# Two FFN up-projections as a seven-product block scheme, with the down-projection as a phase of its own

## The chip, the cores and the metric

The kernel runs on one core of a Trainium2 chip. Five engines take part. TensorE (PE in the rows, PEld its weight loads) multiplies, VectorE (DVE), ScalarE (ACT) and GpSimd (POOL) work element by element, and SyncE (SP) issues nearly all transfers. The metric is the device time of one execution in microseconds, as the median of several executions.

## The reference

A decoder trunk over 1024 tokens of 1024 values: two layers, each a mixer (differential attention with spatial gating in layer 0, a width-31 convolution module in layer 1) and then a gated FFN, which the change is about:

```python
def conv_ffn(h, w_up, dw_w, dw_b, w_down):
    hh = causal_dwconv(h @ w_up, dw_w, dw_b)   # width 3 over tokens, [1024, 5632]
    a, gate = jnp.split(hh, 2, axis=-1)
    return (a * jax.nn.silu(gate)) @ w_down    # [1024, 2816] @ [2816, 1024]

for l in range(2):
    h = rms_norm(x, norm_mix_g[l])
    x = x + (even_mixer if l == 0 else odd_mixer)(h, ...)
    x = x + conv_ffn(rms_norm(x, norm_ffn_g[l]), ffn_w_up[l], ffn_dw_w[l], ffn_dw_b[l], ffn_w_down[l])
return rms_norm(x, final_norm_g)
```

## The kernel before

**Products.** All is in fp32. Every factor is split into two parts hi and lo (`split_hi_lo`: a cast on ACT or DVE, a subtraction on POOL or DVE), and a product of 128x128 weights with 512 columns is three matmuls (hi hi, hi lo, lo hi; `PASSES`). The tokens are two chunks of 512. `stream` loads 512 KB of a weight into a `raw` tile (3 of them), and splits each half into a `hl` tile (8 of them).

**FFN.** A hidden group is two pairs of channel tiles (`GRP` = 2), 11 groups for each chunk and layer. For each channel tile `chan_mm` (L283) makes 24 matmuls into one PSUM bank; `up` evacuates them with the width-3 convolution (ACT L535, DVE L538 for the bank's two other taps, DVE L541 for the edge that comes from the chunk before). `up_a` multiplies by the gate (L555) and splits the product. The group is then pending: after the next group's first pair, `down_steps` (L589) multiplies it with its rows of `w_down`, 12 matmuls into a bank for each token tile and half, and adds each bank into the residual stream `xr` in SBUF (DVE L593). Weights are loaded anew for each chunk.

**Order.** Steps are Python closures; `interleave(main, shadow)` spreads one list over another, and a scheduler then fixes each engine's order. The FFN groups are the `main` that other work is spread over: attention of chunk 1 (`att_steps`) over groups 0 to 6 of layer 0, and in layer 1 the width-31 convolution (`dw_steps`: 22 taps on DVE, L713, and 7 on ACT and POOL for each of 8 channel tiles and chunk) with its layer norm (`ln_steps`) over nine groups of layer 0's chunk 1 and seven groups of layer 1's chunk 0:

```python
interleave(ffn_steps(0, 1, hF0, range(2, NG), pend) + down_steps(pend),
           dw_steps(ys[0]) + spread(ln_steps(0, ys[0], acT), 32), 0.0, 0.9)
```

**PSUM.** Eight banks: one `bank2` of two banks, two `sbank`, four `bank`.

## Time and profile before

| what | value |
|---|---|
| three runs | 2275.6, 2278.47, 2281.07 us (median 2278.47) |
| profiled execution | span 2279.0 us, the time that the sums below go by |
| granted TensorE clock | 0.992 on the mean |
| busy: PE, PEld, DVE, ACT, POOL | 97%, 80%, 73%, 45%, 43% of the span |
| transfers | 258.53 MB, 113 GB/s over the span |

The profile is one execution. Its page gives the busy share of each engine; views of the trace give stretches, groups of like instructions, and the chain of work that ended last.

### The profile page before, as it was taken

The numbers are of one execution on the slowest core, as the hardware profiler recorded it, in microseconds if no ns is written. First come the engines' busy times: TensorE is split into PE (matmuls) and PEld (weight loads), VectorE is DVE, ScalarE is ACT, GpSimd is POOL, SyncE is SP. The second block draws the span as 40 slices with busy tenths as digits, with TensorE's granted clock in tenths as the row PEclk, the third lists the DMA queues.
The fourth block names the chain that finished last, engine by engine and source line by source line (L and its number), as shares of the span: only waits on it lengthen the run. The fifth ranks groups of instructions, "written<-read, shape, count | busy, mean of one in ns | idle before, by whom it ended". The sixth has DMA issues, their size and how long they took to land.

```text
span 2279.0 us, 29045 instructions
## 1 busy us (share of the span) xinstructions
PE 2218.6 (97%) x10246; PEld 1817.3 (80%) x10246; DVE 1668.2 (73%) x3076; ACT 1023.1 (45%) x1793; POOL 986.7 (43%) x775
## 2 busy tenths in 40 slices
PE   8999998999999999999999999999999999999998
PEld 6778777888878888787788878887888888788886
DVE  6786658667664658699988777999663757677766
ACT  4455434564543434455434535555343434333333
POOL 3333223332323333587643337877433435334342
PEclk9999999999999999999999999999999999999999
DMA  6746733333443332332332323332332334323331
GB/s 233 220 143 216 232 115 108 115 101 100 132 144 93 108 96 84 105 99 76 101 93 87 94 81 112 109 92 85 102 101 70 119 90 140 100 84 103 101 93 65
DMA packets 315889, 258.53 MB, mean 113 GB/s; under 512 B 10076, under 2 KB 280672, under 8 KB 315232
## 3 DMA queue, kind: packets, MB, share of 16 engines
q1 hardware_dynamic: 309856, 242.00, 34.9%
q0 software_dynamic: 5888, 14.68, 2.0%
q8 instruction: 81, 1.33, 0.2%
q14 instruction: 64, 0.52, 0.1%
HBM read 233.57 MB, written 23.07 MB: 113 GB/s over the span
## 4 chain that ended last, share of the span: by engine, by line
PE 76%; DVE 17%; issue 2%; DMA 2%; ACT 2%; POOL 0%; SPq 0%; ACTq 0%; DVEq 0%; POOLq 0%
PE bank L283 40%; PE bank L589 17%; PE bank L246 13%; DVE sbank L713 5%; DVE s L538 2%; DVE xr L593 1%; PE sbank L439 1%; DVE hl L129 1%; DVE y L163 1%; DVE s L541 1%; DMA raw<-in_ab_w_in 1%; PE bank L201 1%; PE bank L408 1%; DVE s L555 1%; PE bank L405 1%
## 5 line engine op out<-in xcount | busy, mean ns | idle before, releaser
L129 POOL TENSOR_TENSOR hl<-raw,hl 128x512 fp32r<-128x512 f32 x576 | 765.5, 1336 | 1097.3 <-ACT hl L125 977.1
L283 PE MATMUL bank<-big,hl 128*128 128x512 f32 x4992 | 1155.0, 390 | 0.3 <-DVE xr L593 0.2
L283 PEld LDWEIGHTS bank<-big,hl 128*128 128x128 f32 x4992 | 935.3, 188 | 194.2 <-DVE xr L593 1.5
L125 ACT CAST hl<-raw 128x512 fp32r<-128x512 f32 x648 | 394.7, 617 | 469.4 <-PE bank L589 123.6
L589 PE MATMUL bank<-hl,s 128*128 128x512 f32 x2016 | 493.7, 399 | 17.3 <-DVE xr L593 5.8
L589 PEld LDWEIGHTS bank<-hl,s 128*128 128x128 f32 x2016 | 376.3, 189 | 114.6 <-DVE xr L593 10.3
L538 DVE SCALAR_TENSOR_TENSOR s<-bank,dw,s 128x510 f32<-128x510 f32 x352 | 262.5, 746 | 236.4 <-ACT s L535 232.5
L246 PE MATMUL bank<-hl,big 128*128 128x512 f32 x1728 | 421.8, 399 | 7.8 <-DVE s L357 4.5
L246 PEld LDWEIGHTS bank<-hl,big 128*128 128x128 f32 x1728 | 322.5, 191 | 75.7 <-DVE s L357 2.8
L593 DVE TENSOR_TENSOR xr<-bank,xr 128x512 f32<-128x512 f32 x344 | 231.0, 683 | 56.9 <-PE bank L589 54.9
L713 DVE SCALAR_TENSOR_TENSOR sbank<-yb,cw,sbank 128x512 f32<-128x512 f32 x352 | 246.8, 746 | 2.0 <-ACT sbank L702 0.8
L535 ACT ACTIVATE s<-bank,dw 128x512 f32<-128x512 f32 x176 | 136.7, 777 | 135.1 <-PE bank L283 134.7
L710 POOL TENSOR_TENSOR ap<-ap,pr 128x512 f32<-128x512 f32 x112 | 152.0, 1357 | 27.8 <-ACT ap L705 16.7
L129 DVE TENSOR_TENSOR hl<-raw,hl 128x512 fp32r<-128x512 f32 x160 | 152.0, 961 | 12.2 <-ACT hl L125 10.7
L125 ACT CAST s<-s 128x512 fp32r<-128x512 f32 (+1 forms) x116 | 64.0, 561 | 177.5 <-DVE s L555 155.6
L541 DVE SCALAR_TENSOR_TENSOR s<-halo,dw,s 128x2 f32<-128x2 f32 (+1 forms) x176 | 126.9, 721 | 0.0
L709 ACT ACTIVATE pr<-yb,cw 128x512 f32<-128x512 f32 x112 | 80.5, 723 | 48.5 <-POOL ap L710 47.9
L551 ACT ACTIVATE s<-s 128x512 f32<-128x512 f32 x88 | 55.6, 632 | 85.8 <-DVE s L541 47.7
L129 DVE TENSOR_TENSOR s<-s,s 128x512 fp32r<-128x512 f32 x84 | 71.1, 847 | 24.3 <-ACT s L125 23.2
L515 DVE TENSOR_TENSOR xr<-bank,xr 128x512 f32<-128x512 f32 x32 | 22.0, 688 | 85.3 <-PE bank L246 85.3
L555 DVE TENSOR_TENSOR s<-s,s 128x512 f32<-128x512 f32 x88 | 83.7, 951 | 0.7
L163 DVE SCALAR_TENSOR_TENSOR y<-q,v,y 128x1 f32<-128x1 f32 x160 | 73.0, 475 | 2.1
(137 smaller groups left out, 1448.0 us busy)
## 6 DMA issues: line engine op xcount, KB each, us to landing
raw<-in_ffn_w_up SPq DMA_DIRECT2D x176, 512.0 KB
raw<-in_ffn_w_down SPq DMA_DIRECT2D x88, 512.0 KB
raw<-in_ab_w_in SPq DMA_DIRECT2D x64, 256.0 KB
raw<-in_conv_w_in SPq DMA_DIRECT2D x32, 512.0 KB
qd<-s SPq DMA_DIRECT2D x32, 256.0 KB
qk<-qd POOLq DMA_DIRECT2D x8, 1024.0 KB, 8.1
raw<-in_ab_w_out SPq DMA_DIRECT2D x16, 512.0 KB
raw<-in_conv_w_out SPq DMA_DIRECT2D x16, 512.0 KB
```

Of the source, the lines that this page charges most:

```text
L125: nc.scalar.copy(out=hl_hi, in_=raw)
L129: eng.tensor_sub(out=hl_lo, in0=raw, in1=hl_hi.bitcast(F32))
L246: nc.tensor.matmul(ps, lhsT=hT[c][:, sa, d, tok(t)], rhs=units[d][:, sw, :], start=(n == 0), stop=(n == 3 * DT - 1))
L283: nc.tensor.matmul(ps, lhsT=hv[d // 4][:, sw, d % 4, :], rhs=hT[:, sa, d, :], start=(n == 0), stop=(n == 3 * DT - 1))
L535: nc.scalar.activation(out=y, in_=ps, func=AF.Identity, scale=dw[:, 2, ct:ct + 1], bias=dw[:, 3, ct:ct + 1])
L538: nc.vector.scalar_tensor_tensor(out=y[:, sh:], in0=ps[:, :CH - sh], scalar=dw[:, k, ct:ct + 1], in1=y[:, sh:], op0=ALU.mult, op1=ALU.add)
L541: nc.vector.scalar_tensor_tensor(out=y[:, :sh], in0=halo[:, ct, k:2], scalar=dw[:, k, ct:ct + 1], in1=y[:, :sh], op0=ALU.mult, op1=ALU.add)
L555: nc.vector.tensor_tensor(out=ya, in0=ya, in1=yg, op=ALU.mult)
L589: nc.tensor.matmul(ps, lhsT=ph[:, sa, k * P:(k + 1) * P], rhs=wd[half][:, sw, :], start=(n == 0), stop=(n == 3 * len(phs) - 1))
L593: nc.vector.tensor_add(out=xt, in0=ps, in1=xt)
L710: nc.gpsimd.tensor_add(out=st["ap"], in0=st["ap"], in1=pr)
L713: nc.vector.scalar_tensor_tensor(out=st["acc"], in0=ys[ct][:, k:k + CH], scalar=cw[:, ct, k:k + 1], in1=st["acc"], op0=ALU.mult, op1=ALU.add)
```

## The change

**Seven products.** The up-projection of a pair (channel tiles of the gate `g` and of the value `v`, both chunks, K in two halves) is a 2x2 by 2x2 block product, which before takes eight block products of 12 matmuls. After, it takes seven, of sums and differences of the blocks (Winograd's form of Strassen's scheme). `combos` makes the activations' sums once for each layer from the residual stream, which `norm_steps` has spilled to DRAM (`xd`), and transposes them (tiles T1 to T3, and one over half of `hT[1]`); `pair_steps` makes the weights' sums, the seven products and the outputs' sums. The outputs lie in rows of 1024 tokens, so that the convolution runs over both chunks at once, with no edge. A pair's weights are loaded once, and no longer once for each chunk.

**Which pairs.** The first 6 pairs of layer 0 and 8 of layer 1 stay plain (`head_steps`): chunk 0's before the mixer's end, chunk 1's over the `combos`. The other 16 and 14 pairs take the new form.

**Down-projection.** The gated units go to DRAM (`phd`). When all pairs are done, `down_steps` runs for each chunk and half of the columns: 11 steps, each of which streams 512 KB of `w_down` and 512 KB of `phd`, splits both, and makes 24 matmuls into four banks that accumulate over all steps. The residual is read back from DRAM.

**Order.** Attention of chunk 1 now lies over the first output projection, the norm, two gating products and four plain pairs; the width-31 convolution of chunk 0 over its own input projection and the down-projection of chunk 1, that of chunk 1 over the output projection, its input projection and six plain pairs. Layer norm and RMS norm of one chunk stand side by side between the down-projection and the next input projection. PSUM is re-opened with two `bank2` and two `bank` for the attention of chunk 1. Some mixer tiles get buffers of their own (`held`, `sec`), and the constants' transposes move forward into layer 0's products.

```diff
-DOWN_ENGINES = (("act", "pool"), ("dve", "dve"))
+DOWN_ENGINES = (("act", "pool"), ("act", "pool"))
+PH_ENGINES = (("act", "dve"), ("act", "dve"))
+WRAW = 4
+PRE0, PRE0_LATE = 6, 2
+PRE1, PRE1_LATE = 8, 2
...
+    def combos(l, hT, up_pool):
...
+            for c in range(2):
+                t = c * TPC + k
+                xt = up_pool.tile([P, D], F32, tag="row", name="xa", bufs=ROWS)
+                nc.sync.dma_start(out=xt, in_=xd[l][t * P:(t + 1) * P, :])
+                nc.vector.scalar_tensor_tensor(out=xt, in0=xt, scalar=rn[l][:, t:t + 1], in1=T["gain"],
+                                               op0=ALU.mult, op1=ALU.mult)
+                xs.append(xt)
+            xa, xb = xs
+            nc.vector.tensor_sub(out=xa[:, :512], in0=xb[:, :512], in1=xa[:, :512])
+            nc.gpsimd.tensor_sub(out=xb[:, :512], in0=xb[:, 512:], in1=xb[:, :512])
+            nc.vector.tensor_sub(out=xb[:, 512:], in0=xb[:, 512:], in1=xa[:, :512])
+            nc.gpsimd.tensor_sub(out=xa[:, 512:], in0=xa[:, 512:], in1=xb[:, 512:])
+            for i, src in ((1, xa[:, :512]), (3, xb[:, :512]), (2, xb[:, 512:])):
+                turn(src, T[i][:, 0, :, tok(k)], T[i][:, 1, :, tok(k)])
...
+    def pair_steps(l, hT, T, js, up_pool):
...
+        def product(ps, n, hv, start, stop):
+            i = 0
+            for d in range(4):
+                for sw, sa in PASSES:
+                    nc.tensor.matmul(ps, lhsT=hv[:, sw, d, :], rhs=B[n](sa, d), start=(start and i == 0),
+                                     stop=(i == 11), skip_group_check=True)
+                    i += 1
+        def conv(r, ct):
+            y = s4([P, S])
+            nc.scalar.activation(out=y, in_=r[:, 2:], func=AF.Identity, scale=dw[:, 2, ct:ct + 1], bias=dw[:, 3, ct:ct + 1])
+            for k in (1, 0):
+                nc.vector.scalar_tensor_tensor(out=y, in0=r[:, k:k + S], scalar=dw[:, k, ct:ct + 1], in1=y,
+                                               op0=ALU.mult, op1=ALU.add)
+            return y
...
+            a1 = part(g1, "pool")
+            nc.vector.tensor_add(out=s, in0=v1, in1=v2)
+            a5 = part(s, "dve")
+            nc.vector.tensor_sub(out=v1, in0=g1, in1=v1)
+            nc.vector.tensor_sub(out=s, in0=s, in1=g1)
+            a6 = part(s, "dve")
+            nc.gpsimd.tensor_sub(out=s, in0=g2, in1=s)
+            a3 = part(s, "pool")
+            a7 = part(v1, "pool")
+            a2 = part(g2, "pool")
+            a4 = part(v2, "pool")
+            rg, rv_ = row(), row()
+            A, C = bank(), bank()
+            product(A, 1, a1, True, False)
+            p1 = s2([P, CH])
+            nc.scalar.copy(out=p1, in_=A)
+            product(C, 5, a5, True, False)
+            p5 = s2([P, CH])
+            nc.scalar.copy(out=p5, in_=C)
+            product(A, 6, a6, False, False)
+            u2 = s2([P, CH])
+            nc.scalar.copy(out=u2, in_=A)
+            product(C, 3, a3, False, True)
+            nc.vector.tensor_add(out=rg[:, 2 + CH:], in0=C, in1=u2)
+            product(A, 7, a7, False, False)
+            nc.vector.tensor_add(out=rv_[:, 2 + CH:], in0=A, in1=p5)
+            Bk = bank()
+            product(Bk, 2, a2, True, True)
+            nc.vector.tensor_add(out=rg[:, 2:2 + CH], in0=Bk, in1=p1)
+            yg = conv(rg, HT + j)
+            nc.scalar.activation(out=yg, in_=yg, func=AF.Silu)
+            product(A, 4, a4, False, True)
+            nc.scalar.copy(out=rv_[:, 2:2 + CH], in_=A)
+            yv = conv(rv_, j)
+            nc.vector.tensor_tensor(out=yv, in0=yv, in1=yg, op=ALU.mult)
+            nc.sync.dma_start(out=phd[l][:, j, :], in_=yv)
...
+    d1, ci = d1[4:], conv_in_steps(0, hC, ys[0], True)
+    run([ci[0], d1[0], ci[1], d1[1]])
+    interleave([f for pair in zip(ci[2:], d1[2:8]) for f in pair] + d1[8:], dw_steps(ys[0]), 0.0, 1.0)
+    ci = conv_in_steps(1, hC, ys[1])
+    run([f for pair in zip(norm_steps(1, xtile, norm_mix_g[1], hC, hb=sbank), ln_steps(0, ys[0], acT)) for f in pair])
+    run(ci[:4])
+    dws1 = dw_steps(ys[1])
+    interleave(out_steps(conv_w_out[0], acT, 0, lambda c: None, out_bias(0)) + ci[4:], dws1[:len(dws1) // 2], 0.0, 1.0)
+    interleave(norm_steps(0, xtile, norm_ffn_g[1], hF1, keep=rn[1], spill=xd[1]) +
+               head_steps(1, 0, hF1, range(PRE1 - PRE1_LATE)),
+               dws1[len(dws1) // 2:] + spread(ln_steps(1, ys[1], acT), 16), 0.0, 0.9)
```

**What the scheduler makes of it.** TensorE before, in layer 1's FFN: two channel tiles' banks of 24 matmuls (L283), then the pending group's products with `w_down` (L589).

```order
L283 MATMUL bank_18758<-big_15714,hl_18752 128x512 x12
L283 MATMUL bank_18758<-big_15714,hl_18755 128x512 x12
L283 MATMUL bank_18798<-big_15714,hl_18792 128x512 x12
L283 MATMUL bank_18798<-big_15714,hl_18795 128x512 x12
L589 MATMUL bank_18833<-hl_18736,s4_18584 128x512 x3
L589 MATMUL bank_18833<-hl_18744,s4_18731 128x512 x3
L589 MATMUL bank_18841<-hl_18739,s4_18584 128x512 x3
L589 MATMUL bank_18841<-hl_18747,s4_18731 128x512 x3
```

TensorE after, in layer 0's pairs (L642; `big` and `t` tiles hold the activations, one `hl` tile is one product's weights):

```order
L642 MATMUL bank_7112<-big_5619,hl_7105 128x512 x12
L642 MATMUL bank_7255<-t12_5909,hl_7229 128x512 x2
L642 MATMUL bank_7324<-big_3768,hl_7244 128x512 x2
L642 MATMUL bank_7254<-t12_5910,hl_7234 128x512 x12
L642 MATMUL bank_7324<-big_3768,hl_7244 128x512 x9
L642 MATMUL bank_7255<-big_5619,hl_7238 128x512 x12
L642 MATMUL bank_7324<-big_3768,hl_7244 128x512
L642 MATMUL bank_7254<-t3_5911,hl_7241 128x512 x12
L642 MATMUL bank_7396<-big_3768,hl_7367 128x512 x12
L642 MATMUL bank_7397<-t12_5909,hl_7371 128x512 x11
L642 MATMUL bank_7254<-big_5619,hl_7247 128x512 x12
L642 MATMUL bank_7397<-t12_5909,hl_7371 128x512
```

A bank now gets 12 matmuls at a time, with evacuations between: in bank 7254 the seventh product (the `t3` row) and the fourth (the last row but one) stand 23 matmuls apart, which are the first and most of the fifth product of the next pair.

VectorE before, the same place in layer 1's FFN:

```order
L538 SCALAR_TENSOR_TENSOR s2_18438<-bank_18413,dw1_2972,s2_18438 128x510
L541 SCALAR_TENSOR_TENSOR s2_18438<-halo1_2993,dw1_2972,s2_18438 128x2
L538 SCALAR_TENSOR_TENSOR s2_18438<-bank_18413,dw1_2972,s2_18438 128x511
L541 SCALAR_TENSOR_TENSOR s2_18438<-halo1_2993,dw1_2972,s2_18438 128x1
L538 SCALAR_TENSOR_TENSOR s2_18478<-bank_18453,dw1_2972,s2_18478 128x510
L541 SCALAR_TENSOR_TENSOR s2_18478<-halo1_2993,dw1_2972,s2_18478 128x2
L538 SCALAR_TENSOR_TENSOR s2_18478<-bank_18453,dw1_2972,s2_18478 128x511
L541 SCALAR_TENSOR_TENSOR s2_18478<-halo1_2993,dw1_2972,s2_18478 128x1
L555 TENSOR_TENSOR s2_18478<-s2_18478,s2_18438 128x512
L129 TENSOR_TENSOR s4_18485<-s2_18478,s4_18485 128x512
```

VectorE after, about one pair in layer 0 (`row` holds 1024 tokens of one output, `raw` and `s2` the weights and their sums):

```order
L689 TENSOR_TENSOR row_7534<-bank_7608,s2_7552 128x512
L144 TENSOR_TENSOR hl_7660<-s2_7650,hl_7660 128x512
L686 TENSOR_TENSOR row_7536<-bank_7538,s2_7566 128x512
L650 SCALAR_TENSOR_TENSOR s4_7622<-row_7534,dw0_438,s4_7622 128x1024 x2
L650 SCALAR_TENSOR_TENSOR s4_7640<-row_7536,dw0_438,s4_7640 128x1024
L662 TENSOR_TENSOR s2_7792<-raw_7789 128x512
L650 SCALAR_TENSOR_TENSOR s4_7640<-row_7536,dw0_438,s4_7640 128x1024
L664 TENSOR_TENSOR raw_7789<-raw_7788,raw_7789 128x512
L144 TENSOR_TENSOR hl_7797<-s2_7792,hl_7797 128x512
L695 TENSOR_TENSOR s4_7640<-s4_7640,s4_7622 128x1024
L665 TENSOR_TENSOR s2_7792<-s2_7792,raw_7788 128x512
L684 TENSOR_TENSOR row_7676<-bank_7681,s2_7722 128x512
```

The short edge instructions are gone, and most instructions now have both inputs in SBUF, five of them over 1024 columns.

TensorE before, in layer 1's mixer, around the layer norm of chunk 0 (L740 and L755 are its transposes):

```order
L755 MATMUL sbank_10921<-ident_84,yn_10919 128x128 x4
L755 MATMUL sbank_10933<-ident_84,yn_10919 128x128 x4
L740 MATMUL bank2_11143<-ident_84,yb_8633 128x128
L740 MATMUL bank2_11143<-ident_84,yb_8705 128x128
L740 MATMUL bank2_11143<-ident_84,yb_8777 128x128
L740 MATMUL bank2_11143<-ident_84,yb_8849 128x128
L589 MATMUL bank_10832<-hl_10684,s4_10475 128x512 x3
L589 MATMUL bank_10832<-hl_10692,s4_10667 128x512 x3
L589 MATMUL bank_10847<-hl_10681,s4_10475 128x512 x3
L589 MATMUL bank_10847<-hl_10689,s4_10667 128x512 x3
L589 MATMUL bank_10855<-hl_10684,s4_10475 128x512 x3
L589 MATMUL bank_10855<-hl_10692,s4_10667 128x512 x3
```

TensorE after, at the same layer norm (L893 and L908; L209 are transposes of the RMS norm of chunk 1):

```order
L209 MATMUL sbank_11676<-ident_87,xn_11674 128x128 x4
L209 MATMUL sbank_11683<-ident_87,xn_11674 128x128 x4
L893 MATMUL bank2_11775<-ident_87,yb_9989 128x128
L893 MATMUL bank2_11775<-ident_87,yb_10100 128x128
L893 MATMUL bank2_11775<-ident_87,yb_10211 128x128
L893 MATMUL bank2_11775<-ident_87,yb_10358 128x128
L893 MATMUL bank2_11775<-ident_87,yb_10505 128x128
L893 MATMUL bank2_11775<-ident_87,yb_10651 128x128
L893 MATMUL bank2_11775<-ident_87,yb_10771 128x128
L893 MATMUL bank2_11775<-ident_87,yb_10945 128x128
L908 MATMUL sbank_11721<-ident_87,yn_11719 128x128 x4
L908 MATMUL sbank_11733<-ident_87,yn_11719 128x128 x4
```

Before, FFN matmuls stand between the transposes; after, there are none from the last matmul of the down-projection to the first of the next input projection.

## Rows read from the trace of the kernel before

**Rows 1.** The profile page: span, and its part 1, busy time by engine.

```profile
span 2279.0 us, 29045 instructions
PE 2218.6 (97%) x10246; PEld 1817.3 (80%) x10246; DVE 1668.2 (73%) x3076; ACT 1023.1 (45%) x1793; POOL 986.7 (43%) x775
```

**Rows 2.** Chain that ended last, 2010 to 2060 us: start us, us, what.

```profile
2015.85 21.77 PE bank L283 x96
2037.61 11.24 PE bank L589 x48
```

**Rows 3.** Groups by line and shape, TensorE: count | busy us, mean ns | idle before.

```profile
L283 PE MATMUL bank<-big,hl 128*128 128x512 f32 x4992 | 1155.0, 390 | 0.3 <-DVE xr L593 0.2
L589 PE MATMUL bank<-hl,s 128*128 128x512 f32 x2016 | 493.7, 399 | 17.3 <-DVE xr L593 5.8 <-DVE s L541 4.8 <-DVE s L538 2.0
...
L589 PE MATMUL bank<-hl,ph 128*128 128x512 f32 x96 | 22.8, 397 | 0.0
...
L201 PE MATMUL bank<-ident,xn 128*128 128x128 f32 x128 | 16.6, 272 | 0.6 <-DVE big L205 0.6
```

**Rows 4.** Groups by line and shape, the other engines.

```profile
L129 POOL TENSOR_TENSOR hl<-raw,hl 128x512 fp32r<-128x512 f32 x576 | 765.5, 1336 | 1097.3 <-ACT hl L125 977.1 <-PE bank L589 45.6 <-DVE xr L593 17.3
L125 ACT CAST hl<-raw 128x512 fp32r<-128x512 f32 x648 | 394.7, 617 | 469.4 <-PE bank L589 123.6 <-PE bank L283 112.6 <-PE bank L246 85.2
L713 DVE SCALAR_TENSOR_TENSOR sbank<-yb,cw,sbank 128x512 f32<-128x512 f32 x352 | 246.8, 746 | 2.0 <-ACT sbank L702 0.8
L593 DVE TENSOR_TENSOR xr<-bank,xr 128x512 f32<-128x512 f32 x344 | 231.0, 683 | 56.9 <-PE bank L589 54.9
L129 DVE TENSOR_TENSOR hl<-raw,hl 128x512 fp32r<-128x512 f32 x160 | 152.0, 961 | 12.2 <-ACT hl L125 10.7
L555 DVE TENSOR_TENSOR s<-s,s 128x512 f32<-128x512 f32 x88 | 83.7, 951 | 0.7
L163 DVE SCALAR_TENSOR_TENSOR y<-q,v,y 128x1 f32<-128x1 f32 x160 | 73.0, 475 | 2.1
L173 ACT ACTIVATE big<-xr 128x1024 fp32r<-128x1024 f32 x24 | 25.3, 1055 | 13.6 <-DVE xr L593 10.5 <-PE bank L246 3.1
L352 ACT COPY s<-bank 128x512 f32<-128x512 f32 x32 | 17.4, 591 | 23.7 <-PE bank L351 15.2 <-issue 5.5 <-DMA qd<-s 3.0
L428 DVE SCALAR_TENSOR_TENSOR e<-e,cf 128x1024 f32<-128x1024 f32 x4 | 5.1, 1284 | 0.1
```

**Rows 5.** Timeline, 2160 to 2165 us: start us, us, engine, line, instruction.

```profile
2160.16 1.29 POOL L129 TENSOR_TENSOR hl<-raw,hl 128x512 fp32r<-128x512 f32 x1 [2.04 <-ACT hl L125]
2160.27 1.19 DVE L541 SCALAR_TENSOR_TENSOR s<-halo,dw,s 128x2 f32<-128x2 f32 x1
...
2162.16 0.21 DVE L541 SCALAR_TENSOR_TENSOR s<-halo,dw,s 128x1 f32<-128x1 f32 x1
2162.26 1.29 POOL L129 TENSOR_TENSOR hl<-raw,hl 128x512 fp32r<-128x512 f32 x1 [0.81 <-ACT hl L125]
2162.41 1.68 DVE L555 TENSOR_TENSOR s<-s,s 128x512 f32<-128x512 f32 x1
...
2164.78 0.69 DVE L129 TENSOR_TENSOR s<-s,s 128x512 fp32r<-128x512 f32 x1 [0.69 <-ACT s L125]
```

**Rows 6.** Stretches: us; busy PE, PEld, DVE, ACT, POOL; clock; DMA share, GB/s.

```profile
0.00:382.00 382.00, 352.21 (x1778) 287.44 (x1779) 268.40 (x739) 172.09 (x380) 112.78 (x111) 0.97 0.59 185
382.00:684.00 302.00, 298.48 (x1503) 247.37 (x1502) 203.09 (x373) 162.47 (x279) 91.78 (x71) 1.00 0.37 116
937.00:1340.00 403.00, 393.80 (x1741) 320.17 (x1740) 349.29 (x565) 197.02 (x323) 227.63 (x175) 1.00 0.31 93
1026.00:1083.00 57.00, 54.19 (x239) 43.97 (x238) 57.00 (x90) 31.54 (x49) 40.21 (x30) 1.00 0.26 77
2223.00:2279.00 56.00, 46.13 (x200) 37.14 (x198) 34.67 (x81) 20.41 (x39) 13.95 (x11) 0.94 0.19 66
```

**Rows 7.** DMA issues: KB each, median us from issue to landing.

```profile
qk<-qd POOLq DMA_DIRECT2D x8, 1024.0 KB, 8.1
```

286 lines of the change are left out of this document (170 added, 116 removed).

## The prediction

> **What bounds the kernel now.** I read the page first: TensorE is busy for 2218.6 of 2279.0 us, VectorE for 73%, ScalarE for 45%, GpSimd for 43% [rows 1]. A busy TensorE need not be at its peak, so next comes the chain of waits, in order of time: in a plain FFN stretch it does not leave TensorE, 96 matmuls of L283 take 21.77 us and 48 of L589 take 11.24 us, then the next 96 begin [rows 2]. That is 0.2268 us and 0.2342 us from start to start, where the groups give a mean of 390 and 399 ns for one [rows 3], so matmuls overlap and the time goes with their number. The granted clock there is 1.00, the 2.4 GHz level [rows 6]. So the reader is to see a kernel that is bound by its count of matmuls, with some 60 us in which TensorE waits: 29.8 us of them in the first 382 us, 9.2 us where VectorE carries the convolution (busy for 57.00 of 57 us in its middle), 9.9 us at the tail [rows 6]. Whatever cuts the count counts in full; whatever then leaves TensorE without work is paid in full too.
>
> **The change part by part.** The sum goes against the profiled execution, 2279.0 us, 0.5 us above the median of the runs.
>
> Fewer matmuls: 30 pairs (16 and 14) go from 8 to 7 products of 12, which is 360 matmuls at 0.2268 us [rows 2], **-81.6 us**. If the new ones ran as slowly as L589's (both of whose factors are small tiles) all 2520 of them would cost 0.0074 us more, 18.6 us in all; their moving factor is a large tile as in L283, so I take nothing.
>
> New transposes: three sums and the late one, 4 blocks each, 4 token tiles, 2 layers are 128, exactly the count of L201, busy 16.6 us [rows 3]: **+16.6 us**, none of it covered, as it is TensorE's own.
>
> Down-projection: 2112 matmuls before (2016 and 96 [rows 3]) and after, both factors small tiles, so 0.2342 us as now: **0**. At L283's rate it would be -15.6.
>
> The pairs' other engines, for each pair's 84 x 0.2268 = 19.05 us on TensorE. GpSimd: 6 x 1.336 = 8.0. ScalarE: 7 casts x 0.617, 4 copies x 0.591, 3 of 1024 columns x 1.055, 9.8 in all. VectorE: 3 weight sums x 0.951, 2 lo parts x 0.961, 3 PSUM sums x 0.683, and 5 of 1024 columns x 1.284 (the convolution's form with both inputs in SBUF is L428's; the gate's product goes by it too), 13.2 in all [rows 4]. All are hidden below 19.05. What is late next: the fourth product waits for VectorE's sum out of the seventh, 23 matmuls or 5.2 us earlier; I take 0.2 us for each pair, **+6**. The bounds are nothing and the sum of VectorE and GpSimd, 21.2 - 19.05 = 2.2 for each, +65.
>
> That sum has a reason. Under a GpSimd instruction of 1.29 us a two-column VectorE instruction takes 1.19 us and one of 512 columns 1.68; without one, 0.21 and 0.69. The first ends with GpSimd's, and the second 0.54 us after it [rows 5]. So a VectorE instruction with both inputs in SBUF stands still while GpSimd's runs. Alone, a pair's VectorE work is 5 x 0.69 + 3 x 0.683 + 5 x 1.284 = 11.9; stopped by all six of GpSimd it is 19.9, 0.85 over TensorE, +26 for 30 pairs. The Trainium skill (SBUF — State Buffer, section Who interferes with whom) says that a VectorE instruction with two SBUF inputs and a GpSimd instruction that reads SBUF share a port pair, and the later one fully blocks; the rows agree. By it alone the sum would carry those 26 us in place of 6.
>
> Sums of the activations (`combos`): VectorE has two scalings, two subtractions and three lo parts for each of four steps, 2 x 1.284 + 2 x 0.951 + 3 x 0.683 = 6.5 us [rows 4], under 288 matmuls (65 us): hidden. The late transposes stand alone, four turns through two banks of a 0.591 copy and a 0.683 subtraction, some 2 us for each layer: **+4**; without cover for the rest, 26 us for each layer.
>
> Down-projection as a phase: a step has 24 matmuls, 5.62 us, over 4 x 0.617 = 2.5 on ScalarE, 2.7 on GpSimd, 1.9 on VectorE [rows 4]. Four `raw` tiles are two steps, so a tile must turn in 11.2 us: load and split. 1 MB (a step's two loads) landed 8.1 us after its issue at the dear end, from GpSimd's queue [rows 7]; with two casts and two GpSimd splits (3.9) that is 12.0, 0.4 over for each of 88 steps, +35; at the cheap end nothing, since the first 382 us moved 185 GB/s on the mean [rows 6] and a step wants 187. These transfers stand on SP's queue, not GpSimd's, so I take **+3**. What a step waits behind on SP's queue is the step before it, and the read of the residual, which is wanted only 60 us later.
>
> Layer 0's first part: the constants and the second query product move under other work and held tiles get their own buffers, against 29.8 us of waits [rows 6]: between 0 and -15, **-8**.
>
> Attention of chunk 1: VectorE has 203 of 302 us there now [rows 6]. Before it lay over seven groups (7 x 33.0 = 231 us), after over 24 steps of 24 matmuls (131 us); with the rest of TensorE's 298.5 that is 198 us. VectorE sheds the groups' evacuations and gets the norm and the gates instead. If its 203 stayed whole, it would be over by 5, with chains of softmax steps behind it; from 0 to +25, **+8**.
>
> Layer 1's mixer: the convolution of chunk 0 lay over nine groups (297 us), now over 6 x 48 x 0.2268 + 20 x 24 x 0.2342 = 178 us. VectorE's share there: half of L713's 246.8, 40 lo parts x 0.961, some 24 PSUM instructions x 0.683, 178 [rows 4]: level, as in the middle now, where VectorE's 57.00 of 57 cost TensorE 2.8 [rows 6], so no worse than the 9.2 paid today. Then the layer norm and RMS norm of four tiles stand without matmuls, as the order shows: two roots (each two of 0.475 and smaller ones, some 2 us), a scaling 1.284, six of 0.683 are 9.4 for each tile [rows 4], 38 us against TensorE's 96 transposes at 0.13, 12.5; at most 25 uncovered, and some of it begins under the last steps: **+11**. Chunk 1: VectorE's second half (62 + 38 + 24 for six pairs' evacuations) meets 78 us of TensorE, 45 short, but the stretch ahead has 131 us of matmuls over 73 of VectorE and can take it: between 0 and +45, **+7**.
>
> Tail: the last bank's four token tiles now end together, where before each had its own 24 matmuls; three more roots of 2 us, half hidden: **+3** on 9.9 us.
>
> Sum: -81.6 + 16.6 + 6 + 4 + 3 - 8 + 8 + 11 + 7 + 3 = -31, 2279 - 31 = **2248 us**.
>
> **The rivals.** *Nothing is given back*: the waits stay as they are, -65 alone, or -88 with the first part's and the down-projection's gain: 2191 to 2225. For it, waits are only 3% now with VectorE as full in places; against it, the uncovered norms. *The covers run out*: attention and mixer at their upper ends, 17 + 14 + 38 more: 2317; it turns against the change where they exceed mine by 31. VectorE at 57.00 of 57 speaks for it, its fall of 344 to 32 evacuations at L593's 0.683 against it. *VectorE bounds the pairs*, which ends on the other side: it also waits for the fourth product's copy and scaling before it can go on, some 4 us in each pair by the order (7.9 us of matmuls, 0.591, 1.055, against 5 to 6 us of its own). If GpSimd uses none of that wait, a pair is 19.9 + 4 = 23.9, +4.85 or +146; if it uses all, 19.9. In the middle 21.9, 30 x 2.85 = +86 in place of 6: 2328. It decides from 20.3 us for each pair (19.05 + 0.2 + 31/30). The Trainium skill's rule on the shared ports, above, speaks for this one. *The down-projection waits for transfers*: +35 in place of 3, 2280, no change. That the count does not fall is excluded by the order.
>
> **How the numbers follow.** What a measurement of this kernel tells from no change is 0.2%, 4.6 us. Chances: forecast 0.52 (2225 to 2273), nothing given back 0.18, covers run out 0.12, VectorE bounds the pairs 0.11, transfers 0.07. The range leaves out a quarter of the second (0.05) and most of the third's and fourth's upper parts (0.10): 2205 to 2310; the likeliest case's own is 2225 to 2270. Faster: the first two and a little of the others, 0.73. Same: 0.06. Slower: 0.21.
>
> **What would show it.** TensorE's 30 pairs in 19.0 to 19.5 us each, with starts 0.227 us apart; VectorE near 70% in them; down-projection steps of 5.6 us with no wait for `raw`; a hole of 10 to 25 us on TensorE at chunk 0's layer norm; waits on VectorE in attention below 25 us. The prediction is wrong if a pair takes over 20 us, if steps wait for DMA, or if the mixer's holes add to more than 50 us.

## The result, and the profile after

The changed kernel takes 2318.76 us (2315.81 to 2324.56) against 2279.77 us: a ratio of 1.0174, interval 1.0156 to 1.0192. It is slower by 39 us, where I forecast 31 us faster, and lies outside my range.

The page of the changed kernel, span and busy time by engine, answers to [rows 1]:

```profile
span 2316.3 us, 28698 instructions
...
PE 2171.3 (94%) x10014; PEld 1781.0 (77%) x10014; DVE 1598.2 (69%) x2654; ACT 1130.6 (49%) x1993; POOL 1124.9 (49%) x879
...
PEclk9989979999999999999999979979989999999999
```

TensorE is busy for 47 us less and idle for 145 us in place of 60. The third line is its granted clock in forty slices; before, every digit was a 9.

For a table by stretch I use one measure. TensorE's *own work* is its instructions times the spacing at which each kind follows the last where nothing is waited for: 0.227 us for 512 columns, 0.109 for 128, 0.233 for L589. What a stretch takes *beyond* that is its length less its own work; it holds waits and time at half clock alike. The same code in two profiles can differ in it by some 4 us over the first thousand.

| Work | beyond, before | beyond, after | more | I took |
|---|---|---|---|---|
| layer 0's first part and attention, to the first pair | 58.3 | 103.9 | +45.6 | -8, +8, +4 |
| other FFN products and down-projections | 8.4 | 10.5 | +2.1 | +6, +3 |
| chunk 0's convolution | 13.2 | 13.0 | 0 | 0 |
| layer norm of chunk 0, norm of chunk 1 | (in the row above) | 31.1 | +31.1 | +11 |
| chunk 1's convolution, its output projection, both FFN norms | 6.0 | 42.7 | +36.7 | +7 |
| tail | 9.8 | 13.0 | +3.2 | +3 |
| TensorE's own work | 2183.0 | 2102.3 | -80.8 | -65 |

The sum is +37.7, against +37.3 between the spans. The same stretches of the changed kernel, with columns as in [rows 6]:

```profile
0.00:322.00 322.00, 266.47 (x1339) 217.84 (x1340) 198.98 (x533) 136.44 (x319) 87.20 (x91) 0.92 0.61 191
322.00:684.00 362.00, 347.77 (x1800) 290.35 (x1799) 255.43 (x560) 177.06 (x321) 112.43 (x86) 0.99 0.44 140
684.00:992.00 308.00, 307.94 (x1352) 252.65 (x1351) 205.43 (x215) 152.29 (x230) 153.31 (x128) 1.00 0.29 94
992.00:1335.00 343.00, 336.02 (x1475) 271.44 (x1474) 265.10 (x356) 178.24 (x305) 241.46 (x172) 1.00 0.51 161
1335.00:1377.00 42.00, 20.04 (x91) 16.59 (x90) 32.12 (x103) 27.65 (x54) 10.32 (x9) 0.63 0.30 87
1377.00:1498.00 121.00, 121.00 (x540) 100.26 (x539) 106.46 (x175) 68.62 (x112) 94.10 (x71) 1.00 0.37 112
1498.00:1545.00 47.00, 31.13 (x130) 25.04 (x129) 46.45 (x63) 28.37 (x42) 38.06 (x29) 0.75 0.19 56
...
1660.00:1706.00 46.00, 36.56 (x161) 29.59 (x160) 38.49 (x57) 17.27 (x27) 23.02 (x17) 0.85 0.40 118
1790.00:2046.00 256.00, 255.94 (x1124) 209.94 (x1123) 169.62 (x175) 126.23 (x191) 129.92 (x109) 1.00 0.26 83
2046.00:2303.00 257.00, 253.01 (x1110) 207.37 (x1109) 143.37 (x158) 114.02 (x213) 139.89 (x94) 1.00 0.59 203
```

The reader is to see that the new form itself runs as meant: in the pairs (third and ninth row) TensorE is busy for all but 0.1 us at full clock, with VectorE at 67%. The loss stands in the first row and in rows five, seven and eight, each with the clock under 1.00. What TensorE waits for in the last three of these, by the waits of PE from 1335 to 1377 us, and from 1498 to 1706 us:

```profile
PE sbank L209 <- DVE v L169: 9.7, 1, 9.7
PE sbank L908 <- ACT yn L902: 5.5, 2, 4.2
```

```profile
PE bank L217 <- DVE big L221: 20.1, 4, 5.5
PE bank L265 <- ACT big L140: 3.0, 3, 1.8
```

L209 and L217 are, in these stretches, transposes of a norm's token tiles. Nothing else is queued on TensorE there, so it stands through the chain of each tile on the other engines. The longest such wait, in the timelines of TensorE, VectorE and GpSimd around 1340 us (start us, us, instruction, in brackets the idle time before it):

```profile
1347.50 1.94 PE L209 MATMUL sbank<-ident,xn 128*128 128x128 f32 x8 [9.65 <-DVE v L169]
...
1341.76 2.37 DVE L178 SCALAR_TENSOR_TENSOR y<-q,v,y 128x1 f32<-128x1 f32 x2
...
1344.24 1.10 DVE L178 SCALAR_TENSOR_TENSOR y<-q,v,y 128x1 f32<-128x1 f32 x1
...
1345.33 0.33 DVE L178 SCALAR_TENSOR_TENSOR y<-q,v,y 128x1 f32<-128x1 f32 x2
...
1336.70 8.62 POOL L144 TENSOR_TENSOR hl<-raw,hl 128x512 fp32r<-128x512 f32 x7
```

While GpSimd makes the lo parts of the next weights, until 1345.3 us, a one-column step of a root takes VectorE some 1.1 us; right behind, two take 0.33. The Trainium skill (SBUF — State Buffer, section Who interferes with whom) has these two kinds of instruction exclude each other, and the trace agrees. The three slow steps take 3.47 us of the 9.65; whether the hole shrinks when GpSimd's work is moved away from there was not tried.

In the first part, the end of the attention of chunk 0 (TensorE, then VectorE):

```profile
293.90 0.75 PE L377 MATMUL bank<-identr,held 128*128 128x128 f32 x4 [5.37 <-DVE s L359]
...
301.97 0.75 PE L373 MATMUL bank<-identr,s 128*128 128x128 f32 x4 [6.67 <-ACT s L374]
...
302.11 0.69 DVE L379 COPY sec<-bank 128x512 f32<-128x512 f32 x1 [7.07 <-DMA kd<-sec]
```

`flush()` works off all held second halves of query products at once, with no matmul of a product between. The last row is a copy into the one `sec` buffer, which waits 7.07 us for the store of the tile before.

### The profile page after: what moved, and what is told of

It is laid out like the page before. It is cut to its first block, busy times and chain, and to the rows that moved or that the text cites. A ratio compares the mean times of both kernels' runs of the same rounds, so it can differ in the third digit from the quotient of the medians.

```text
span 2316.3 us, 28698 instructions
## 1 busy us (share of the span) xinstructions
PE 2171.3 (94%) x10014; PEld 1781.0 (77%) x10014; DVE 1598.2 (69%) x2654; ACT 1130.6 (49%) x1993; POOL 1124.9 (49%) x879
## 4 chain that ended last, share of the span: by engine, by line
PE 70%; DVE 17%; issue 4%; ACT 3%; POOL 3%; DMA 2%; SPq 0%; ACTq 0%; DVEq 0%; POOLq 0%
PE bank L642 25%; PE bank L721 15%; PE bank L302 13%; PE bank L265 12%; DVE sbank L866 5%; DVE hl L144 2%; DVE y L178 2%; POOL ap L863 1%; PE sbank L461 1%; POOL hl L144 1%; DVE xn L193 1%; ACT hl L140 1%; PE sbank L209 1%; PE bank L430 1%; PE sbank L609 1%
## 5 line engine op out<-in xcount | busy, mean ns | idle before, releaser
L302 PE MATMUL bank<-big,hl 128*128 128x512 f32 x2112 | 499.6, 395 | 9.0 <-DVE big L221 3.0
L721 PE MATMUL bank<-hl 128*128 128x512 f32 x2112 | 489.2, 391 | 8.3 <-DVE hl L144 6.5
L721 PEld LDWEIGHTS bank<-hl 128*128 128x128 f32 x2112 | 393.9, 188 | 98.9 <-DVE hl L144 15.2
L302 PEld LDWEIGHTS bank<-big,hl 128*128 128x128 f32 x2112 | 396.5, 190 | 94.8 <-ACT big L220 4.9
L144 DVE TENSOR_TENSOR hl<-raw,hl 128x512 fp32r<-128x512 f32 x248 | 276.1, 1139 | 197.9 <-ACT hl L140 197.5
L642 PE MATMUL bank<-big,hl 128*128 128x512 f32 x1440 | 345.5, 390 | 0.1
L642 PEld LDWEIGHTS bank<-big,hl 128*128 128x128 f32 x1440 | 269.8, 188 | 59.0 <-POOL hl L144 1.0
L650 DVE SCALAR_TENSOR_TENSOR s<-row,dw,s 128x1024 f32<-128x1024 f32 x120 | 198.2, 1652 | 156.9 <-ACT s L648 153.0
L642 PE MATMUL bank<-t,hl 128*128 128x512 f32 x1080 | 265.3, 392 | 0.0
L642 PEld LDWEIGHTS bank<-t,hl 128*128 128x128 f32 x1080 | 202.5, 188 | 44.2
L556 DVE SCALAR_TENSOR_TENSOR s<-bank,dw,s 128x510 f32<-128x510 f32 x112 | 83.5, 745 | 57.0 <-ACT s L553 55.5
L862 ACT ACTIVATE pr<-yb,cw 128x512 f32<-128x512 f32 x112 | 80.8, 723 | 71.9 <-POOL ap L863 71.7
L648 ACT ACTIVATE s<-row,dw 128x1024 f32<-128x1024 f32 x60 | 74.9, 1248 | 12.2 <-DVE row L689 10.0
```

Of the source, the lines that this page charges most:

```text
L144: eng.tensor_sub(out=hl_lo, in0=raw, in1=hl_hi.bitcast(F32))
L302: nc.tensor.matmul(ps, lhsT=hv[d // 4][:, sw, d % 4, :], rhs=hT[:, sa, d, :], start=(n == 0), stop=(n == 3 * DT - 1))
L556: nc.vector.scalar_tensor_tensor(out=y[:, sh:], in0=ps[:, :CH - sh], scalar=dw[:, k, ct:ct + 1], in1=y[:, sh:], op0=ALU.mult, op1=ALU.add)
L642: nc.tensor.matmul(ps, lhsT=hv[:, sw, d, :], rhs=B[n](sa, d), start=(start and i == 0), stop=(i == 11), skip_group_check=True)
L648: nc.scalar.activation(out=y, in_=r[:, 2:], func=AF.Identity, scale=dw[:, 2, ct:ct + 1], bias=dw[:, 3, ct:ct + 1])
L650: nc.vector.scalar_tensor_tensor(out=y, in0=r[:, k:k + S], scalar=dw[:, k, ct:ct + 1], in1=y, op0=ALU.mult, op1=ALU.add)
```

## The experiments

Ratios are to the kernel before, in runs on the same chip; the changed kernel stands at 1.0174. All change the changed kernel unless said otherwise.

**The pairs as plain products.**

```diff
-            first, last, T = combos(l, hT, up_pool)
-            interleave(head_steps(l, 1, hT, range(pre)), first, 0.0, 0.6)
-            run(last)
-            run(pair_steps(l, hT, T, range(pre, HT), up_pool))
+            run(head_steps(l, 1, hT, range(pre)))
+            for j in range(pre, HT):
+                run(head_steps(l, 0, hT, [j]) + head_steps(l, 1, hT, [j]))
```

> The changed kernel with the 30 pairs as plain products: 8 instead of 7 for each, and no sums of the activations. That is 360 matmuls of 512 columns more and 128 transposes fewer. Theory (the seven products pay their full price, and what was lost was lost elsewhere): 360 x 0.227 - 128 x 0.109 = +67.8 us on the changed kernel's 2318.8, so 2380 to 2392, and the waits outside the pairs stay where they are. Rival (the pairs or the sums of the activations themselves lose time, which plain products would not): less than +55, below 2374.

1.0390 (1.0361 to 1.0418), 2371.14 us: below both 2374 and the theory's range. TensorE's own work grows by 67.7 us, as worked out, but 16 us less are lost beyond it, 12.5 of them between the heads and the end of the pairs of both layers (4.2 and 8.3). The rival's condition is met: the seven products are worth some 50 us here, not 68. The 12.5 us lie in the stretch with the second norm, the sums of the activations and the pairs; which of their waits goes with the pairs was not tried alone. The hole at the layer norm (31.1) and chunk 1's convolution (28.1) stay as they are.

**VectorE's capacity or the order, chunk 1.** First, taps left out:

```diff
-            dtaps = list(range(1 + POOL_TAPS, PAD))
+            dtaps = list(range(1 + POOL_TAPS, last))
...
-    dws1 = dw_steps(ys[1])
+    dws1 = dw_steps(ys[1], 19)
```

> The changed kernel with 11 of VectorE's 22 taps left out in the convolution of chunk 1 alone, which takes 8 x 11 x 0.746 = 66 us off VectorE between 1377 and 1700 us. In that stretch TensorE stands about 42 us beyond its own work. Theory of capacity (VectorE has more work there than TensorE has matmuls beside it): at least 30 us of the 42 go, 2276 to 2289. Theory of order (tiles of a norm follow each other with no matmul between them, each waiting for VectorE once): the waits at the norm tiles get shorter but stay, less than 15 us go, 2304 to 2316.

1.0145 (1.0121 to 1.0168), 2315.69 us. With 66 us less on VectorE the norm tiles still stand 3 to 7 us apart without a matmul, and only 6 of the 27.9 us beyond own work between the fourth input product and the end of the output projection go. Theory of order, so far. Then the order alone:

```diff
-    interleave(out_steps(...) + ci[4:], dws1[:len(dws1) // 2], 0.0, 1.0)
-    interleave(norm_steps(0, ...) + head_steps(1, 0, ...), ...)
+    nf = norm_steps(0, ...)
+    interleave(out_steps(...) + [f for pair in zip(ci[4:], nf) for f in pair], dws1[:len(dws1) // 2], 0.0, 1.0)
+    interleave(head_steps(1, 0, ...), ...)
```

> The changed kernel with the four tiles of chunk 0's norm for the second FFN placed between the last four input products of chunk 1's convolution (48 matmuls between one tile and the next), instead of one after the other behind them. Nothing is left out. Theory of order: the 21.7 us that TensorE loses between 1498 and 1545 us go nearly all, 2296 to 2304. Theory of capacity: VectorE's work stays, so the wait appears again some matmuls later, and less than 8 us of the total go, 2311 to 2319.

1.0154 (1.0128 to 1.0180), 2318.40 us, no gain: the hole at the norms falls from 21.7 to about 10 us, and 17 us are lost between 1579 and 1640 us, where it was 7. Theory of capacity, by itself. Both together, so with half of the taps left out:

> Both edits at once: half of VectorE's taps left out in chunk 1's convolution, and the norm tiles of chunk 0 between the last input products. The first alone took 6 us off the stretch from the fourth input product to the end of the output projection of chunk 1 (27.9 us beyond TensorE's own work), the second 1.3 us. Theory (two limits, one behind the other: the serial chain of each norm tile where it stands without matmuls, and VectorE's capacity where it doesn't): only both together free the stretch, it falls to less than 10 us, 2294 to 2302 in all. Rival (a third thing, such as one two-bank tile and one norm tile for the whole chain, keeps the norm tiles slow wherever they stand): the stretch stays above 18 us, 2308 to 2316.

1.0077 (1.0060 to 1.0094), 2302.08 us: 11.5 us beyond, in place of 27.9: just over what the theory of two limits gave, far from the rival's 18. So there are two limits, one behind the other, and either alone hides the other. The second edit with more plain products as cover, nothing left out:

```diff
-PRE1, PRE1_LATE = 8, 2
+PRE1, PRE1_LATE = 12, 2
```

> The changed kernel with 12 instead of 8 of layer 1's output tiles made by plain products (8 products more under chunk 1's convolution, 4 pairs fewer) and the norm tiles between the last input products. Nothing is left out. Theory (VectorE's work in that stretch needs more matmuls beside it; with taps left out the same order freed it): the stretch from the fourth input product to the end of the output projection loses less than 12 us beyond TensorE's work in place of 27.9, and 4 x 12 x 0.227 = 10.9 us are paid for the pairs, so a gain of 3 to 8 us, a ratio of 1.014 to 1.016. Rival (the stretch stays above 20 us): slower by 5 to 11 us, 1.019 to 1.022.

1.0121 (1.0098 to 1.0144), 2308.16 us, 8.5 us beyond. The theory holds, and the gain is larger than it said. The order alone left 26.6 us there, so the 10.9 us for four pairs buy back 18; in the totals that is 1.0154 to 1.0121, and the two intervals overlap. TensorE and VectorE in that stretch, changed kernel and this one:

```profile
1377.00:1654.00 277.00, 256.93 (x1153) 210.52 (x1152) 217.82 (x369) 154.46 (x255) 181.72 (x137) 0.96 0.33 104
```

```profile
1375.00:1676.00 301.00, 294.51 (x1344) 244.44 (x1343) 230.71 (x395) 172.70 (x284) 203.71 (x154) 0.99 0.36 115
```

TensorE is idle for 6.5 us in 301, where it was 20 in 277.

**The hole at the layer norm.** The layer norm under the last down-projection steps:

```diff
-    interleave(... + d1[8:], dw_steps(ys[0]), 0.0, 1.0)
+    interleave(... + d1[8:], dw_steps(ys[0]) + spread(ln_steps(0, ys[0], acT), 16), 0.0, 1.0)
-    run([f for pair in zip(norm_steps(1, ...), ln_steps(0, ys[0], acT)) for f in pair])
+    run(norm_steps(1, ...))
```

> The changed kernel with the four layer norm tiles of chunk 0 no longer interleaved with the RMS norm of chunk 1 but placed under the last steps of the down-projection, right behind the convolution's taps. Nothing is left out. TensorE loses 31 us between 1335 and 1377 us. Theory of order: half of the work of that stretch finds matmuls beside it and the hole falls to 12 to 18 us, so 2301 to 2308. Theory of capacity: VectorE is busy for 59.9 of 60 us in the stretch ahead of it, so the taps end later or the layer norm does not get in, and less than 6 us go, 2313 to 2319.

1.0239 (1.0211 to 1.0266), 2335.65 us: worse than either expected. The taps end no earlier, the layer norm does not get in, and now norm and layer norm follow each other, 49 us beyond in place of 31. With half of VectorE's taps left out in chunk 0:

> As the earlier edit that put the layer norm of chunk 0 under the last steps of the down-projection (which made the hole 49 us instead of 31, since the taps did not end earlier), and half of VectorE's taps left out in chunk 0's convolution, 66 us of VectorE's work. Theory of capacity (the layer norm could not get in because VectorE was full with taps until the last step): now it gets in, the hole falls to the norm's 12 to 20 us, 2301 to 2311, 1.009 to 1.014. Rival (the layer norm waits for something else than VectorE's taps, such as GpSimd's seven taps for each tile): the hole stays above 40 us, 2325 to 2335.

1.0146 (1.0131 to 1.0161), 2314.66 us. Half of the layer norm's transposes now stand ahead of the last down-projection matmul, and 18 of the 49 us go; 31.6 remain, between the two expectations, two layer norm tiles and four norm tiles in a row. So capacity is a part; the rest is argued to be the serial chain of these tiles, which was not changed by itself. Last, the layer norm under the next input products:

```diff
+    run(norm_steps(1, ...))
+    interleave(ci[:4], ln_steps(0, ys[0], acT), 0.0, 1.0)
```

> The changed kernel with the RMS norm of chunk 1 alone behind the down-projection and the four layer norm tiles of chunk 0 under the first four input products of chunk 1's convolution (192 matmuls, 43.6 us) instead of zipped with the norm. Nothing is left out. TensorE stands 31 us beyond its own work in that place now, most of it at half clock. Theory (the layer norm has no matmul beside it, and VectorE, which has 12 us in 60 free right behind, can do it there): the hole falls to 12 to 18 us, 2303 to 2311, a ratio of 1.010 to 1.014 to the kernel before. Rival (the norm's four tiles alone take as long, since each is a chain through one norm tile, and the products then wait for VectorE): the hole stays above 25 us, no gain, 1.016 to 1.019.

1.0268 (1.0250 to 1.0286), 2341.48 us. The hole falls by 10 us to 21.4, but the stretch behind loses 33 more; by the waits of PE there, the second layer norm now waits for taps that come late:

```profile
PE bank L893 <- DVE yb L870: 19.6, 2, 10.4
PE bank L217 <- DVE big L221: 18.7, 3, 10.0
```

What one place gains VectorE owes at the next. Both expectations missed this.

**The first part.** Four edits, one at a time:

```diff
+    run(gate_steps(1, 0))
     flush()
```

> The changed kernel with the first gate product of chunk 1 (four token tiles, 96 matmuls of 512 columns, 21.8 us) moved back to where it stood before the change: ahead of the point at which the held second halves of the query products are all worked off, and so ahead of the output projection of chunk 0. Nothing is left out. Up to the first head product TensorE stands 98.7 us beyond its own work (a little over 50 us in the kernel before), 25 us of it between 282 and 322 us, where transposes of held tiles follow one another with no matmul between. Theory (that hole is the missing cover): 10 to 20 us go there, 2299 to 2309. Rival (the gate's matmuls are then missing under the attention of chunk 1, whose chains of softmax steps give it back): less than 5 us in all, 2314 to 2322.

1.0181 (1.0165 to 1.0196), 2326.74 us: by the ratio no gain, as the rival said, though the time is above its 2322. By stretch, the hole at 282 us shrinks from 25 to 7 us, the output projection 20 us later then waits 13, and the attention and heads behind it lose 8 more.

```diff
-    interleave([... gate_steps(0, 1), norm_steps(1, ...) ...], const_steps())
+    run([... gate_steps(0, 1), norm_steps(1, ...) ...])
...
+    run(const_steps())
     flush()
```

> The changed kernel with the 17 small constants (tap rows turned into columns) no longer spread under the gate products of the start but in one piece behind the query products, where they stood before the change. Nothing is left out. Between 60 and 161 us TensorE stands 25 us beyond its own work, and 13.5 us in the kernel before. Theory (the constants' loads stand on SP's queue among the weights and their transposes stop TensorE, so spreading them cost about 10 us): 60 to 161 us loses 8 to 12 us less, and as they now stand bare behind the query products the whole gains 0 to 8 us, 2311 to 2319. Rival (they are too small to matter in either place, and the losses there have another cause): the lag of that stretch stays within 4 us of 25, and the total rises, since the piece has no matmul beside it, 2320 to 2332.

1.0137 (1.0122 to 1.0152), 2315.28 us. Up to the end of layer 0's pairs 4 us are gained (102.5 beyond for 106.3); seven other profiles, whose code is the changed kernel's up to there, lie up to 3.4 us below it too, so the place of the gain is not shown. The total is the theory's, but the stretch that I named keeps 23 of its 25 us, as the rival said: the constants were not what is lost there.

```diff
-tag="sec", name="sec", bufs=1
+tag="sec", name="sec", bufs=2
```

> The changed kernel with two buffers in place of one for the tiles in which the second half of a query or gate product is put together and stored from (to make room a small tile of the layer norm has two buffers in place of three). Nothing is left out. In the changed kernel VectorE waits there for the store of the tile before, 7.1 us at the worst. Theory (the one buffer makes the held second halves wait for each other's stores): 5 to 15 us of the 98.7 us before the first head product go, 2304 to 2314. Rival (the wait lies beside others, the four-column query tiles' three buffers above all, which are as they were): less than 3 us, 2316 to 2321.

1.0120 (1.0103 to 1.0136), 2311.87 us: 10.9 us less before the first head product, 7.6 to 11 against all the profiles that share that part with the changed kernel. The theory holds.

> The changed kernel with the order of layer 0's first part as it stood before the change: attention of chunk 0 over twelve steps, then the last query product, the constants in one piece, the first gate product of chunk 1, and then the output projection; and two buffers for the tiles of the second halves. Nothing is left out. Up to the first head product TensorE stands 98.7 us beyond its own work in the changed kernel; in the kernel before it was 52 up to its first FFN product and 6 under the attention of chunk 1. Theory (the 40 us come from this order and the one buffer): the stretch falls to 60 to 75 us, 2283 to 2303 in all, a ratio of 1.003 to 1.011. Rival (they come from what this leaves as it is: the attention of chunk 1 that has only 24 steps of small cover, the forced working-off of all held tiles, the deeper weight buffers): the stretch stays above 85 us, 1.012 to 1.018.

1.0130 (1.0101 to 1.0158), 2311.65 us. To the first head product some 20 us are gained, short of the theory, and 10 of them lost again behind it, 6.5 in one wait at 516 us, where the second output projection's input comes back from DRAM. Order and buffer together give no more than the buffer alone. Then more cover for that attention, 12 plain output tiles in layer 0 (`PRE0, PRE0_LATE = 12, 2`):

> The changed kernel with 12 instead of 6 of layer 0's output tiles made by plain products, eight head products of which lie under the attention of chunk 1 in the changed kernel and twenty now. Nothing is left out. Six pairs fewer cost 6 x 12 x 0.227 = 16.3 us. TensorE stands 15 us beyond its own work between 402 and 490 us, under that attention. Theory (the attention lacks matmuls beside it): the lag there falls below 5 us, so 4 to 8 us slower in all than the changed kernel, a ratio of 1.019 to 1.021. Rival (it does not depend on the cover): the whole 16 us are paid, 1.023 to 1.026.

1.0265 (1.0246 to 1.0284), 2341.43 us: all of the 16 us are paid, and nothing comes back, 108.7 us beyond up to the end of layer 0's pairs in place of 106.3. The attention of chunk 1 does not lack matmuls.

**Edits together.** Two `sec` buffers, late constants, 12 plain tiles in layer 1, the second norm spread:

> Four edits together, nothing left out: two buffers for the tiles of the second halves (0.54% faster alone), the constants in one piece (0.37%), the norm tiles between the input products with 12 plain output tiles in layer 1 (0.53%), and the norm of chunk 1 over four to five head products in place of two (up to 0.3%, by the 14.6 us lost there). Theory (these are separate holes of TensorE, so the gains add): a ratio of 0.997 to 1.004 to the kernel before, where the changed kernel is at 1.017. Rival (the holes are one shortage that moves from place to place): 1.008 to 1.014.

1.0172 (1.0153 to 1.0190), 2318.03 us, worse than either expectation. In layer 1 the gains add (8.6 us beyond in the convolution of chunk 1, and 7 us less from there to the end of the pairs). In the first part they do not: two edits that gain 10 us and at most 4 alone lose 15 together, 121.6 us beyond up to the end of the pairs. Its longest wait, by the waits of PE up to 640 us, is for the attention's output to come back from DRAM:

```profile
PE bank L217 <- DMA ot<-og: 12.6, 2, 10.8
```

With 14 plain tiles and the layer norm under the input products besides:

> As the four edits together, with 14 plain output tiles in layer 1 (5.4 us more) and the layer norm of chunk 0 under the first four input products of chunk 1's convolution. Nothing is left out. Alone that last edit made the hole behind the down-projection 10 us smaller, and the stretch behind it lost 33 us more, as VectorE's backlog came out at its end. Theory (with more matmuls in that stretch the backlog is covered): 10 us are gained and less than 5 lost there, a ratio of 0.996 to 1.003. Rival (it is not covered by two output tiles more): 1.006 to 1.015.

1.0197 (1.0181 to 1.0213), 2326.09 us, again worse than either. The hole is again 9 us smaller, the stretch behind loses 12 in place of 33 more, the two tiles cost their 5 us: no gain.

**The new form in layer 1 alone.** Layer 0, its FFN and all up to chunk 0's layer norm as in the kernel before, `PRE1, PRE1_LATE = 14, 3`:

```diff
+    interleave(old_ffn(0, 1, hF0, range(2, NG), pend) + old_down(pend),
+               dw_steps(ys[0]) + spread(ln_steps(0, ys[0], acT), 32), 0.0, 0.9)
...
+    interleave(head_steps(1, 0, hF1, range(PRE1 - PRE1_LATE)),
+               dws1[n1:] + spread(ln_steps(1, ys[1], acT), 16), 0.0, 0.95)
...
     ffn_rest(1, hF1, PRE1)
```

> The kernel before in layer 0 and up to the layer norm of layer 1's convolution (FFN groups beside attention and convolution, down-projection in the groups), and the changed form only in layer 1's FFN, behind which nothing waits for cover: 14 plain output tiles beside chunk 1's convolution, then 8 pairs of seven products and the down-projection as a phase. Nothing is left out. TensorE's own work against the kernel before: -8 x 12 x 0.227 = -21.8, 64 transposes +7.0, the down-projection of that layer at 0.227 in place of 0.2342 -7.6, together -22. Theory (the seven products pay where no other engine's work needs matmuls beside it, and all else that was lost was lost cover): 10 to 18 us are given back at the norms and the tail, so 4 to 12 us faster than the kernel before, a ratio of 0.994 to 0.999. Rival (the form itself costs, through its reloads, its spilled rows and its separate phases): 1.003 or more.

0.9998 (0.9985 to 1.0010), 2281.26 us: the loss is gone, the gain too, between theory and rival. In the profile the own work falls by 19.8 us, layer 1 gives back 15 with the tail, as expected, and 13.6 are lost up to 1410 us, where the order is that of the kernel before. That sum is +9, and the medians differ by -2: the profiled execution, 2289.65 us, was the longest of twelve, so a part of the 13.6 is its own.

> The same with 12 plain output tiles and 10 pairs in layer 1: 5.4 us less of TensorE's own work, and 21.8 us less matmul cover beside chunk 1's convolution. Theory (cover decides there: VectorE has some 180 us of work in that stretch, TensorE 185 with 14 tiles and 163 with 12): the 5 us are lost again or more, a ratio of 0.996 to 1.003, above that with 14. Rival (cover is not short with 12): 2 to 5 us faster than with 14.

1.0027 (1.0016 to 1.0038), 2289.89 us: above that with 14 tiles, as the theory of cover said. It isn't shown by this run alone: the edit also puts 55% of chunk 1's convolution steps, in place of 45%, beside the input products, ahead of the plain tiles. Up to 1410 us, with the same code as the run with 14, it loses some 5 us less. For the 13.6 us I tried `WRAW = 3`, `YB = 8`:

> The version with the new form in layer 1 alone and 14 plain output tiles, with three buffers for raw weights and eight rows of the convolution as in the kernel before, in place of four and twelve. Nothing is left out. Up to 1410 us that version follows the order of the kernel before, yet TensorE stands 89 us beyond its own work there in place of 75. Theory (the deeper raw buffers send weights ahead of the attention's loads and stores on SP's queue, which is also a part of the changed kernel's first part): 8 to 14 us come back there, a ratio of 0.993 to 0.997. Rival (the buffers have nothing to do with it, and the pairs, which use two raw tiles each, wait with three): 1.000 to 1.006.

1.0078 (1.0064 to 1.0092), 2303.07 us, above both. Up to 1410 us 9 of the 13.6 come back against the first profile of that code, but only 4 against the second, about as far as these two lie apart; so it is not shown that the sizes did it. The down-projection pays, 26.2 us beyond in place of 4.3. Its stretch with four raw tiles, then with three:

```profile
2050.00:2275.00 225.00, 221.83 (x974) 182.12 (x972) 120.64 (x140) 98.06 (x188) 124.43 (x86) 1.00 0.57 193
```

```profile
2050.00:2289.00 239.00, 222.42 (x938) 175.71 (x936) 74.71 (x136) 98.98 (x186) 107.04 (x84) 0.99 0.55 176
```

The largest wait of PE over the run with three is for ScalarE's casts (L792 is the down-projection here), and these wait for the loads of `phd`: with three tiles, a step's two turn too slowly. The first line is PE's, the others are ScalarE's waits in the two stretches, with three tiles, then with four:

```profile
PE bank L792 <- ACT hl L142: 9.3, 17, 2.5
```

```profile
ACT hl L142 <- DMA raw<-phd: 108.6, 35, 5.5
```

```profile
ACT hl L142 <- DMA raw<-phd: 1.4, 4, 0.9
```

## Why the prediction was wrong

*Fewer matmuls, new transposes.* Right: -81.7 and +13.9 (at 0.109 us, where I took the busy mean).

*Down-projection: 0.* Mis-sized; it gained 12.7. The reading of 0.2342 us was right: the 48 matmuls of L589 in [rows 2] start 0.231 to 0.238 us apart with no wait among them, and over the run the median is 0.234. What was wrong is that the rate would stay because both factors are still small tiles. L721 starts every 0.227 us; in the chain of the changed kernel:

```profile
2077.65 82.57 PE bank L721 x363
```

The value lies near the bound that I gave (-15.6). Why L589's matmuls stand 3% further apart is not known; no run changed it alone.

*The pairs, +6, the sums, +4, the tail, +3, the down-projection's transfers, +3.* Right within 2 us or so: the pairs lose 4.8, the sums some 5; with the pairs as plain products 12.5 us went there. VectorE's stop under GpSimd is there (the 1024-column step of L650 takes 1.65 us on the mean, against 1.28 in [rows 4]) and stays covered. Four raw tiles are needed for the last of these terms; with three one layer alone lost 22 us, which is the rival of the transfers. Two groups of the changed kernel's page:

```profile
L721 PE MATMUL bank<-hl 128*128 128x512 f32 x2112 | 489.2, 391 | 8.3 <-DVE hl L144 6.5
...
L650 DVE SCALAR_TENSOR_TENSOR s<-row,dw,s 128x1024 f32<-128x1024 f32 x120 | 198.2, 1652 | 156.9 <-ACT s L648 153.0
```

*Layer 0's first part, -8, and attention, +8.* This is the step that failed most. Of the 68 us between my 2248 and the profile's 2316.3, 42 are here, 20 at the norms and 30 at chunk 1's convolution; the other terms give 23 back. I priced the moves by the work that each took off or added, and the new buffers as a gain. The order shows three things that I did not price: the held tiles all worked off in one place, one `sec` buffer for what had shared five, and the gates gone from beside both. The `sec` buffer is shown (8 to 11 us). The gates put back gained nothing, and more plain products beside the attention of chunk 1, whose cover I took for the risk, gained nothing either. The rest of the 45.6 us, some 35, is not settled: edits of the order move it, and single gains do not add.

*Norm beside layer norm, +11.* The place was right, the size 31. I priced VectorE's and TensorE's time at full speed, 38 against 12.5. VectorE was busy for 32 of the 42; what I left out is the chain (each tile's steps on ScalarE, VectorE and TensorE wait for one another, as the waits show), and that TensorE ran its transposes at half clock. That the single tiles `xn`, `yn` and `bank2` make the chain so long is argued; none of them was given a second buffer.

*Chunk 1's convolution, +7 of 0 to 45.* It is 36.7. 14.6 of the 42.7 us beyond own work lie behind the convolution, at the norm of chunk 1 under two head products, which I had not priced at all. For the rest I let the excess of VectorE's work flow into the stretch ahead; it did not all do so, since the taps of chunk 1 are issued only behind its first input products: VectorE is busy for 46.45 of 47 us at the norms and for 48 of 60 us a hundred us earlier. And with half the taps left out the stretch still lost 21.9 of 27.9 us, so the norms' order is a limit of its own.

So the rival "the covers run out" had the time (2317) and two of its three places. That the time fits is in part luck: the first part lost 25 us more than its sum has there, and the own work fell by 16 us more. My range ended at 2310 since I cut the upper part of that case.

The mechanism behind two of the three: the FFN's matmuls were what other engines' work stood beside. Products over both chunks can't begin until both chunks are through, so they lie where nothing needs cover (TensorE idle for 0.1 us in 308), and the convolution and norms lie bare. Two runs show it: with 12 plain output tiles and the norm spread between input products chunk 1's convolution loses 8.5 us in place of 27.9, and with the new form in layer 1 alone, where the FFN groups of layer 0 stand beside attention and convolution again, the loss is gone. More cover than that (14 tiles, the layer norm under the input products) gained nothing.

## What to carry to other kernels

Before matmuls are removed or joined into a phase, list what other engines' work stands beside them now, and price that work bare: chain by chain through its single buffers, not as the difference of two sums. Where a bound runs from 0 to 45 and the cover is short by 45, the likely value is not 7. A hole that is made smaller at one place should be looked for at the next before the edit is believed; a run in which two limits are lifted together tells what two single ones can't.

## What the hardware showed

TensorE's clock falls to its lower level (1.2 GHz) in the holes, where it stands idle between short runs of matmuls: granted clocks of 0.63, 0.75 and 0.85 in rows five, seven and eight above. From 1377 to 1498 us, with TensorE busy throughout, it is 1.00. By the mean granted clock, 0.992 over 2279.0 us and 0.970 over 2316.3, it was at that level for 36 us before and 139 us after. In those stretches I summed what each matmul took beyond its spacing, up to twice the spacing: 10 us before, 34 after. So some 24 of the 118 us that are lost beyond own work are not waits but matmuls at half rate. From 1335 to 1377 us the granted clock was 0.63 and TensorE's own work 11 us, while it shows as busy for 20. The Trainium skill (TensorE: Matmul & The Clock Gate, Part 1) says that the throttled state is the default and activity releases it; the trace agrees, with 0.63 in the hole and 1.00 in the busy stretch behind it. No term of the prediction had it.
